# In projection of a hybrid decoder block: three passes of 256 columns become one of 512 and one of 256

## The chip, the cores and the metric

The kernel runs on one core of a Trainium2 chip. The metric is the device time of one execution in microseconds (us), as the median of several runs. All numbers are float32 at the interface.

## The reference, cut to what matters

One layer on x of 256 tokens by 2048 features:

```
proj = x @ w_in                                   # 2048 -> 4688 columns
u_ssm, q, k, v, qi, ki, wi = split(proj)          # 1024, 1024, 256, 256, 1024, 64, 16
y_ssm  = s5_mixer(u_ssm, ...)                     # diagonal state space scan, then a gated unit (GLU)
y_attn = dsa_attention(q, k, v, qi, ki, wi * c)   # indexer picks 64 keys per query, then softmax attention
h = layer_norm(alpha * x + concat(y_ssm, y_attn) @ w_out)
f = (gelu(causal_conv3(h @ w_up)) * (h @ w_gate)) @ w_down
out = layer_norm(alpha * h + f)
```

## The kernel before, in words

Every matrix product keeps nearly float32 accuracy by splitting: a float32 value is written as a high part (rounded to the engine's fp32r type) and a low part (the rest), and a product a*b is taken as high*high + high*low + low*high. Weights come from memory in halves of 128 x 1024 values (eight blocks of 128 input features for 128 output columns). `fetch` (L126) does this for one half: SyncE starts the DMA into `raw`, ScalarE writes `wh` (L133), VectorE writes `wl` (L136). Three `raw` buffers and four each of `wh` and `wl` go round, so a few halves are prepared ahead of TensorE.

x is split in the same way at the start (`load_x`, L224, with `split`, L180): its four tiles hold, for each of 16 blocks of input features, 256 columns (tokens) of the high part and right behind them 256 of the low part. The tiles arrive in this order: half of tile 0, half a weight half, the other halves of both, then tile 1, three weight halves, tile 2, tile 3.

The in projection makes 27 transposed tiles (output columns on partitions, 256 tokens along the row): eight of u for the state space part, eight of qi and one of kw for the indexer, two of k, eight of q. The v columns are done the other way round and are not touched by the change. A transposed tile takes 16 blocks, and for each block `mm3` (L184) issues three passes of 256 columns: high weights on high x (L186), low weights on high x (L187), high weights on low x (L188). All three add up in the same 256 columns of a PSUM bank. The tile is then moved to SBUF by one ScalarE copy (L303, or L315 for u, or at L626 for kw).

The first four u tiles run with all first halves before all second halves, since x's second half comes late. From the fifth on, `ws_tile` (L288) runs a tile, and after every block it calls `pump`, which issues one step of background work: first the state space job `ssm` (four blocks: matmuls `bu`, a long run of VectorE operations L561 to L575 with the results `t1a`, `t2a` or `t12b`, and matmuls L594 on those results), later the indexer (matmuls L650, ScalarE L656, VectorE L661 to L670). The names `t1a` and so on repeat every second block, so "the third block" uses `t1a` and `t2a` again.

The order on each engine is not the order of the code. A scheduler lays out all instructions engine by engine before the run; weight fetches and the moves out of PSUM are marked as of high priority. Each engine then takes its instructions strictly in that order, and waits where an operand is not there yet. Two PSUM banks named `acc` take turns over the tiles.

The up and gate products of the feed-forward part already use another scheme, `wide_half` (L195): since the high and low parts of the activations lie side by side, one pass with the high weights runs over 512 columns (high x in the first 256 columns of the bank, low x in the second 256), and one pass with the low weights runs over the 256 high columns into the first 256. The eight high passes of a half stand together, and so do the eight low ones. Its result lies in two halves of a bank, and is put together by a ScalarE copy (L1046) and a VectorE add (L1047).

Of the kernel before, what the change touches and what calls it, by code (L numbers as in the profile page):

```python
# [11 lines left out]
F32R = mybir.dt.float32r  # L12
# [70 lines left out]
def block_kernel(ctx: ExitStack, tc: tile.TileContext, x_t, x_n, prm_d, cst_d, ssm_d, w_in_d, w_kw_d, w_v_d,  # L83
# [106 lines left out]
    def act_tiles(what):  # L190
        return [(t[:, :, 0, :], t[:, :, 1, :])
                for t in (ahl.tile([P, 4, 2, S], F32R, name=f"{what}{j}", tag=f"hl{j}") for j in range(4))]

    def wide_half(out, half, tiles, kh):


        def passes(low):
            for k in range(8):
                r = tiles[(kh * 8 + k) // 4][:, k % 4]
                yield low, half[low][:, k * P:(k + 1) * P], r[:, 0] if low else r  # L200

        steps = list(passes(1)) + list(passes(0)) if kh else list(passes(0)) + list(passes(1))
        for i, (low, w, r) in enumerate(steps):
            ins = T.matmul(out[:, 0] if low else out, lhsT=w, rhs=r, start=kh == 0 and i == 0, stop=kh == 1 and i == 15)  # L204
        return ins.ins

    def kt_of(tiles, kt):
        h, l = tiles[kt // 4]
        return h[:, kt % 4, :], l[:, kt % 4, :]
# [8 lines left out]
    st = tmp.enter_context(pool("ssmt", side="right"))  # L218
    xt = act_tiles("x")
    raw_b = st.tile([P, 2, 512], F32, name="raw_b", tag="t3")  # L220
# [51 lines left out]
    def acc_tile():  # L272
        return ps.tile([P, 512], F32, name="acc", bufs=2)
# [14 lines left out]
    def ws_tile(evac, m=P):  # L288

        acc = acc_tile()  # L290
        for kt in range(16):
            if kt % 8 == 0:
                half = next_half()
            c = (kt % 8) * m
            mm3(acc[:m, :S], (half[0][:, c:c + m], half[1][:, c:c + m]), kt_of(xt, kt), kt == 0, kt == 15)
            pump()
        with tc.high_priority():
            evac(acc)

    def proj_tile(name, t=None):  # L300
        if t is None:
            t = proj.tile([P, S], F32, name=name)
        ws_tile(lambda acc: A.activation(t, acc[:, :S], AF.Copy))  # L303
        return t
# [8 lines left out]
    def u_tile(ct, acc):  # L313
        t = proj.tile([P, 2, P], F32, name=f"u{ct}")
        A.activation(t.rearrange("p two k -> p k two"), acc[:, :S].rearrange("p (k two) -> p k two", two=2), AF.Copy)  # L315
        ut.append(t)

    bu = psb.tile([P, 2, 2, 512], F32, name="bu")
    accs = [acc_tile(), acc_tile(), bu[:, 0, 0], bu[:, 0, 1]]
    for kh in range(2):  # L320
        for ct in range(4):
# [4 lines left out]
            if (kh, ct) == (1, 3):  # L326
                load_some(raw_c.rearrange("p a b -> p (a b)"), ssm_d[:, 1024:], 0, 1024)
                load_some(cst, cst_d, CST_FIRST, NCST)
            for k in range(8):
                kt = kh * 8 + k  # L330
                c = k * P
                mm3(accs[ct][:, :S], (half[0][:, c:c + P], half[1][:, c:c + P]), kt_of(xt, kt), kt == 0, kt == 15)
            if kh:
# [291 lines left out]
    kw = proj.tile([P, S], F32, name="kw")[0:80]  # L625
    ws_tile(lambda acc: A.activation(kw, acc[:80, :S], AF.Copy), m=80)  # L626
    ki2 = proj.tile([P, S], F32, name="ki2")
# [142 lines left out]

    hl_tiles = [ahl.tile([P, 4, 2, S], F32R, name=f"mix{j}", tag=f"hl{j}") for j in range(4)]
    hl = [(t[:, :, 0, :], t[:, :, 1, :]) for t in hl_tiles]
    mix = [hl[0], hl[1], mix[2], hl[3]]
# [264 lines left out]
    with pool("pd", space=PSUM) as pd:  # L1038
        for f in range(NF):
            pu = []  # L1040
            for which in range(1 if f < 4 else 2):
# [3 lines left out]
                t = ff.tile([P, S], F32, name=f"sum{which}", bufs=2)  # L1045
                A.activation(t, p[:, 1], AF.Copy)  # L1046
                V.tensor_tensor(t, t, p[:, 0], op=ALU.add)  # L1047
                pu.append(t)
# [196 lines left out]
```

## Time and profile before

| what | value |
|---|---|
| median of 3 runs | 1109.63 us (1107.95 to 1109.7) |
| the profiled execution's own time | 1110.08 us |
| its span, first to last instruction | 1108.3 us |
| TensorE (PE) busy | 1089.2 us, 98% |
| VectorE (DVE) busy | 739.4 us, 67% |
| ScalarE (ACT) busy | 578.7 us, 52% |
| DMA | 204.44 MB, mean 184 GB/s |
| mean granted TensorE clock | 0.994 of full |

PE is the engine of matmuls, PEld its weight loads, which overlap with it. Matmul rows overlap each other, because a matmul's duration reaches from its start to the end of its result: the time that a matmul takes of the engine is read from one start to the next, not from its duration. In the same way two VectorE rows that follow each other overlap a little.

### The profile page before, as it was taken

How to read it: one execution, taken by the hardware profiler on the slowest of the kernel's cores; microseconds unless marked ns; L12 is line 12 of the kernel's file. 1: busy time of each engine (PE TensorE's matmuls, PEld its weight loads, DVE VectorE, ACT ScalarE, POOL GpSimd, SP SyncE). 2: the span in 40 equal slices, each digit the busy share in tenths (PEclk: the TensorE clock that was granted, in tenths of full speed). 3: DMA queues.
4: the chain of work that ended last, by engine and by line, in shares of the span. 5: the costliest groups of instructions: out<-in, count | busy, mean ns of one | idle time of the engine just before them, and what ended most of it. 6: DMA issues, size and time to landing. Idle time of an engine off the chain costs nothing.

```text
span 1108.3 us, 16859 instructions
## 1 busy us (share of the span) xinstructions
PE 1089.2 (98%) x6576; PEld 945.8 (85%) x6576; DVE 739.4 (67%) x1044; ACT 578.7 (52%) x876; POOL 0.2 (0%) x4
## 2 busy tenths in 40 slices
PE   8999999999999999999999999999999999999995
PEld 6999998899778788888888888888888888888884
DVE  6979889687558666677666656565656556565547
ACT  5975564457544755555554545454545445454430
POOL 0000000000000000000000000000000000000000
PEclk9999999999999999999999999999999999999998
DMA  7654435346466465555755555555555566665622
GB/s 254 224 154 136 129 132 170 97 140 241 160 221 208 164 201 188 190 189 190 265 191 190 190 191 189 189 191 191 187 190 187 180 229 220 222 222 196 194 100 76
DMA packets 59311, 204.44 MB, mean 184 GB/s; under 512 B 7264, under 2 KB 10080, under 8 KB 58592
## 3 DMA queue, kind: packets, MB, share of 16 engines
q1 hardware_dynamic: 59232, 203.38, 55.2%
q8 instruction: 51, 0.84, 0.3%
q14 instruction: 28, 0.23, 0.1%
HBM read 200.20 MB, written 2.10 MB: 183 GB/s over the span
## 4 chain that ended last, share of the span: by engine, by line
PE 85%; DVE 6%; DMA 3%; ACT 2%; issue 2%; SPq 1%; DVEq 0%; ACTq 0%
PE pd L204 42%; PE e L186 7%; PE e L188 7%; PE e L187 7%; PE o L188 3%; PE o L186 3%; PE o L187 3%; PE acc L187 3%; PE acc L188 3%; PE acc L186 3%; DMA raw<-in_w_in_dram 2%; DVE wl L136 2%; PE misc L650 1%; SPq L530 1%; ACT wh L133 1%
## 5 line engine op out<-in xcount | busy, mean ns | idle before, releaser
L136 DVE TENSOR_TENSOR wl<-raw,wh 128x1024 fp32r<-128x1024 f32 x299 | 364.7, 1222 | 250.1 <-ACT wh L133 247.5
L133 ACT ACTIVATE wh<-raw 128x1024 fp32r<-128x1024 f32 x299 | 315.6, 1056 | 252.2 <-PE pd L204 138.5
L204 PE MATMUL pd<-mix,wh 128*128 128x512 f32 x1344 | 321.4, 391 | 0.7 <-ACT gate L1018 0.7
L204 PEld LDWEIGHTS pd<-mix,wh 128*128 128x128 f32 x1344 | 246.8, 188 | 48.8 <-ACT gate L1018 1.1
L204 PEld LDWEIGHTS pd<-mix,wl 128*128 128x128 f32 x1344 | 172.5, 191 | 6.6
L204 PE MATMUL pd<-mix,wl 128*128 128x256 f32 x1344 | 174.8, 283 | 0.0
L186 PE MATMUL acc<-x,wh 128*128 128x256 f32 (+1 forms) x400 | 115.2, 289 | 2.4 <-ACT x L181 1.6
L187 PE MATMUL acc<-x,wl 128*128 128x256 f32 (+1 forms) x400 | 115.9, 290 | 1.2 <-DVE wl L136 0.8
L188 PE MATMUL acc<-x,wh 128*128 128x256 f32 (+1 forms) x400 | 115.4, 289 | 0.8 <-DVE x L182 0.8
L136 DVE TENSOR_TENSOR wxl<-raw,wxh 128x1024 fp32r<-128x1024 f32 x42 | 51.4, 1225 | 44.6 <-ACT wxh L133 42.6
L186 PEld LDWEIGHTS acc<-x,wh 128*128 128x128 f32 (+1 forms) x400 | 76.8, 193 | 4.7 <-ACT x L181 1.8
L187 PEld LDWEIGHTS acc<-x,wl 128*128 128x128 f32 (+1 forms) x400 | 77.2, 193 | 4.0 <-issue 1.4
L188 PEld LDWEIGHTS acc<-x,wh 128*128 128x128 f32 (+1 forms) x400 | 77.2, 193 | 3.3 <-issue 1.6
L133 ACT ACTIVATE wxh<-raw 128x1024 fp32r<-128x1024 f32 x42 | 44.6, 1061 | 55.9 <-DMA raw<-in_w_down_dram 24.2
L187 PE MATMUL e<-wh,acthl 128*128 128x512 f32 x152 | 59.1, 389 | 0.0
L186 PE MATMUL e<-wh,acthl 128*128 128x512 f32 x152 | 59.0, 389 | 0.0
L188 PE MATMUL e<-wl,acthl 128*128 128x512 f32 x152 | 58.3, 389 | 0.0
L175 ACT ACTIVATE hc<-hc 128x256 f32<-128x256 f32 x44 | 18.4, 417 | 76.4 <-DVE hc L1060 76.4
L186 PE MATMUL e<-wxh,acthl 128*128 128x512 f32 x128 | 49.8, 389 | 0.0
L187 PE MATMUL e<-wxh,acthl 128*128 128x512 f32 x128 | 49.8, 389 | 0.0
L188 PE MATMUL e<-wxl,acthl 128*128 128x512 f32 x128 | 49.8, 389 | 0.0
L1047 DVE TENSOR_TENSOR sum<-sum,pd 128x256 f32<-128x256 f32 x84 | 34.7, 413 | 0.0
(289 smaller groups left out, 1439.4 us busy)
## 6 DMA issues: line engine op xcount, KB each, us to landing
raw<-in_w_gate_dram SPq DMA_DIRECT2D x88, 512.0 KB, 4.1
raw<-in_w_up_dram SPq DMA_DIRECT2D x88, 512.0 KB, 4.0
raw<-in_w_down_dram SPq DMA_DIRECT2D x88, 512.0 KB, 4.6
raw<-in_w_in_dram SPq DMA_DIRECT2D x51, 512.0 KB, 4.3
raw<-in_w_out_dram SPq DMA_DIRECT2D x32, 512.0 KB, 4.1
raw<-in_w_glu_dram SPq DMA_DIRECT2D x8, 512.0 KB, 3.7
raw<-in_w_v_dram SPq DMA_DIRECT2D x4, 512.0 KB, 4.2
z<-in_x_n_dram SPq DMA_DIRECT2D x1, 2048.0 KB, 8.7
```

Source lines behind the costliest of these rows:

```text
L133: A.activation(h[:, :w], raw[:, :w], AF.Copy)
L136: V.tensor_sub(l[:, :w], raw[:, :w], h[:, :w].bitcast(F32))
L175: ins = A.activation(*args, **kw)
L186: T.matmul(out, lhsT=lh[0], rhs=rh[0], start=start, stop=False)
L187: T.matmul(out, lhsT=lh[1], rhs=rh[0], start=False, stop=False)
L188: return T.matmul(out, lhsT=lh[0], rhs=rh[1], start=False, stop=stop).ins
L204: ins = T.matmul(out[:, 0] if low else out, lhsT=w, rhs=r, start=kh == 0 and i == 0, stop=kh == 1 and i == 15)
L530: nc.sync.dma_start(out=ustk[r:r + 32, c, h, :], in_=ut[2 * bi + c][32 * q:32 * q + 32, 1 - e, :])
L650: T.matmul(banks[e][:, (hp % 2) * w:(hp % 2 + 1) * w], lhsT=qit[hp][r, b * 128:(b + 1) * 128], rhs=ki2[r, 0:w], start=True, stop=True)
L1047: V.tensor_tensor(t, t, p[:, 0], op=ALU.add)
```

## The change

The transposed tiles of the in projection go over to the scheme of the up and gate products. `wide_half` gets the tile's width `m` (80 for kw) and a call `beside`, which it makes after each low pass; `ws_tile` passes `pump` there. Each tile then has 16 passes of 512 columns with the high weights and 16 of 256 with the low ones, in runs of eight: in a tile's first half the high ones first, in the second half the low ones first. The move out of PSUM becomes a ScalarE copy and a VectorE add (`add_parts`).

```diff
     def act_tiles(what):
-        return [(t[:, :, 0, :], t[:, :, 1, :])
-                for t in (ahl.tile([P, 4, 2, S], F32R, name=f"{what}{j}", tag=f"hl{j}") for j in range(4))]
-
-    def wide_half(out, half, tiles, kh):
+        return [ahl.tile([P, 4, 2, S], F32R, name=f"{what}{j}", tag=f"hl{j}") for j in range(4)]
+
+    def both_parts(tiles):
+        return [(t[:, :, 0, :], t[:, :, 1, :]) for t in tiles]
+
+    def wide_half(out, half, tiles, kh, m=P, beside=lambda: None):
 
 
         def passes(low):
             for k in range(8):
                 r = tiles[(kh * 8 + k) // 4][:, k % 4]
-                yield low, half[low][:, k * P:(k + 1) * P], r[:, 0] if low else r
+                yield low, half[low][:, k * m:(k + 1) * m], r[:, 0] if low else r
 
         steps = list(passes(1)) + list(passes(0)) if kh else list(passes(0)) + list(passes(1))
         for i, (low, w, r) in enumerate(steps):
             ins = T.matmul(out[:, 0] if low else out, lhsT=w, rhs=r, start=kh == 0 and i == 0, stop=kh == 1 and i == 15)
+            if low:
+                beside()
         return ins.ins
+
+    def two_parts(bank, m=P):
+        return bank[:m].rearrange("p (two s) -> p two s", two=2)
+
+    def add_parts(t, hi, lo):
+        A.activation(t, lo, AF.Copy)
+        V.tensor_tensor(t, t, hi, op=ALU.add)
...
     def ws_tile(evac, m=P):
 
-        acc = acc_tile()
-        for kt in range(16):
-            if kt % 8 == 0:
-                half = next_half()
-            c = (kt % 8) * m
-            mm3(acc[:m, :S], (half[0][:, c:c + m], half[1][:, c:c + m]), kt_of(xt, kt), kt == 0, kt == 15)
-            pump()
+        acc = two_parts(acc_tile(), m)
+        for kh in range(2):
+            wide_half(acc, next_half(), x_tiles, kh, m, pump)
         with tc.high_priority():
             evac(acc)
 
     def proj_tile(name, t=None):
         if t is None:
             t = proj.tile([P, S], F32, name=name)
-        ws_tile(lambda acc: A.activation(t, acc[:, :S], AF.Copy))
+        ws_tile(lambda acc: add_parts(t, acc[:, 0], acc[:, 1]))
         return t
...
     def u_tile(ct, acc):
         t = proj.tile([P, 2, P], F32, name=f"u{ct}")
-        A.activation(t.rearrange("p two k -> p k two"), acc[:, :S].rearrange("p (k two) -> p k two", two=2), AF.Copy)
+        add_parts(t, *(acc[:, i].rearrange("p (k two) -> p two k", two=2) for i in range(2)))
         ut.append(t)
 
     bu = psb.tile([P, 2, 2, 512], F32, name="bu")
-    accs = [acc_tile(), acc_tile(), bu[:, 0, 0], bu[:, 0, 1]]
+    accs = [two_parts(a) for a in (acc_tile(), acc_tile(), bu[:, 0, 0], bu[:, 0, 1])]
...
-            for k in range(8):
-                kt = kh * 8 + k
-                c = k * P
-                mm3(accs[ct][:, :S], (half[0][:, c:c + P], half[1][:, c:c + P]), kt_of(xt, kt), kt == 0, kt == 15)
+            wide_half(accs[ct], half, x_tiles, kh)
...
-    ws_tile(lambda acc: A.activation(kw, acc[:80, :S], AF.Copy), m=80)
+    ws_tile(lambda acc: add_parts(kw, acc[:, 0], acc[:, 1]), m=80)
```

The scheduler lays the program out anew. On PE, the first half of the first tile, right behind the warming matmuls, starts like this before (`x_81` is x's tile 0, `x_82` its tile 1):

```order
L186 MATMUL acc<-x_81,wh 128x256
L187 MATMUL acc<-x_81,wl 128x256
L188 MATMUL acc<-x_81,wh 128x256
L186 MATMUL acc<-x_81,wh 128x256
L187 MATMUL acc<-x_81,wl 128x256
L188 MATMUL acc<-x_81,wh 128x256
```

and like this after, where the first four rows are the whole half and the next four the half after it:

```order
L206 MATMUL acc<-x_81,wh 128x512 x4
L206 MATMUL acc<-x_82,wh 128x512 x4
L206 MATMUL acc<-x_81,wl 128x256 x4
L206 MATMUL acc<-x_82,wl 128x256 x4
L206 MATMUL acc<-x_81,wh 128x512 x4
L206 MATMUL acc<-x_82,wh 128x512 x4
```

The low passes on tile 0 of x now stand behind the high passes on tile 1, and every high pass reads both parts of x.

On VectorE, in the third block of the state space job, the order from the scan into `t2a` to the result `t1a` and a little beyond is this before (L568 is a scan, L570 to L574 the turning back, `t_1256` and `t_1257` are work tiles):

```order
L568 SCALAR_TENSOR_TENSOR t2a<-dec,t1a 128x1024
L569 SCALAR_TENSOR_TENSOR t_1257<-dec,t_1256 128x1024
L570 TENSOR_TENSOR t1a<-t2a,cs 128x1024
L136 TENSOR_TENSOR wl<-raw,wh 128x1024
L571 TENSOR_TENSOR t_1256<-t_1257,cs 128x1024
L573 TENSOR_TENSOR t2a<-t2a,cs 128x1024
L572 TENSOR_TENSOR t1a<-t1a,t_1256 128x1024
L136 TENSOR_TENSOR wl<-raw,wh 128x1024
L574 TENSOR_TENSOR t_1257<-t_1257,cs 128x1024
```

and this after (five lines further down in the code; L216 is the new add, here of the k tiles):

```order
L573 SCALAR_TENSOR_TENSOR t2a<-dec,t1a 128x1024
L216 TENSOR_TENSOR kv<-kv,acc 128x256
L574 SCALAR_TENSOR_TENSOR t_1116<-dec,t_1115 128x1024
L136 TENSOR_TENSOR wl<-raw,wh 128x1024
L575 TENSOR_TENSOR t1a<-t2a,cs 128x1024
L576 TENSOR_TENSOR t_1115<-t_1116,cs 128x1024
L578 TENSOR_TENSOR t2a<-t2a,cs 128x1024
L136 TENSOR_TENSOR wl<-raw,wh 128x1024
L577 TENSOR_TENSOR t1a<-t1a,t_1115 128x1024
```

One add and one more weight conversion stand between the scan and `t1a`, and each add waits there for the ScalarE copy of a tile that TensorE has finished.

## Rows read from the trace of the kernel before

**Rows 1.** The page: the span, busy time, and the chain that ended last.
```profile
span 1108.3 us, 16859 instructions
...
PE 1089.2 (98%) x6576; PEld 945.8 (85%) x6576; DVE 739.4 (67%) x1044; ACT 578.7 (52%) x876; POOL 0.2 (0%) x4
...
PE 85%; DVE 6%; DMA 3%; ACT 2%; issue 2%; SPq 1%; DVEq 0%; ACTq 0%
```
**Rows 2.** The three longest waits of PE from 25 to 230 us: total, times, longest.
```profile
PE acc L186 <- ACT kv L691: 0.9, 1, 0.9
PE acc L187 <- DVE wl L136: 0.8, 2, 0.5
PE bu L186 <- ACT u L315: 0.4, 1, 0.4
```
**Rows 3.** Stretches: length, busy us of PE, PEld, DVE, ACT, POOL; PE clock, DMA.
```profile
75.00:100.00 25.00, 24.49 (x306) 22.38 (x305) 25.00 (x23) 17.02 (x34) 0.00 (x0) 1.00 0.40 124
100.00:125.00 25.00, 25.00 (x281) 22.80 (x281) 23.79 (x20) 12.26 (x29) 0.00 (x0) 1.00 0.48 142
```
**Rows 4.** Groups by line and form: the L186 passes of the transposed tiles.
```profile
L186 PE MATMUL acc<-x,wh 128*128 128x256 f32 x384 | 110.7, 290 | 2.4 <-ACT x L181 1.6 <-ACT kv L691 0.9
L186 PE MATMUL bu<-x,wh 128*128 128x256 f32 x32 | 9.2, 286 | 0.4 <-ACT u L315 0.4
L186 PE MATMUL acc<-x,wh 128*80 128x256 f32 x16 | 4.5, 282 | 0.0
```
**Rows 5.** PE in order of time (start us, us), 48 passes apart.
```profile
109.35 0.28 PE L186 MATMUL acc<-x,wh 128*128 128x256 f32 x1
...
115.11 0.28 PE L186 MATMUL acc<-x,wh 128*128 128x256 f32 x1
```
**Rows 6.** PE in order of time, in the up and gate products.
```profile
504.54 3.82 PE L204 MATMUL pd<-mix,wh 128*128 128x512 f32 x16
508.19 2.08 PE L204 MATMUL pd<-mix,wl 128*128 128x256 f32 x16
510.11 3.82 PE L204 MATMUL pd<-mix,wh 128*128 128x512 f32 x16
```
**Rows 7.** Groups by line: moves out of PSUM, here and in the feed-forward part.
```profile
L1047 DVE TENSOR_TENSOR sum<-sum,pd 128x256 f32<-128x256 f32 x84 | 34.7, 413 | 0.0
L1046 ACT ACTIVATE sum<-pd 128x256 f32<-128x256 f32 x84 | 30.4, 362 | 0.0
L303 ACT ACTIVATE q<-acc 128x256 f32<-128x256 f32 x8 | 3.1, 385 | 9.8 <-PE acc L188 9.8
```
**Rows 8.** PE in order of time, at the start.
```profile
9.47 0.28 PE L188 MATMUL acc<-x,wh 128*128 128x256 f32 x1
11.31 0.38 PE L186 MATMUL acc<-x,wh 128*128 128x256 f32 x1 [1.56 <-ACT x L181]
12.57 0.38 PE L188 MATMUL acc<-x,wh 128*128 128x256 f32 x1 [0.76 <-DVE x L182]
```
**Rows 9.** VectorE at the same time: the low part of x's tile 1.
```profile
11.29 1.23 DVE L182 TENSOR_TENSOR x<-xraw,x 128x1024 fp32r<-128x1024 f32 x1
```
**Rows 10.** Stretches at the start, columns as in rows 3.
```profile
12.50:16.20 3.70, 3.63 (x18) 3.63 (x19) 3.21 (x11) 1.08 (x2) 0.00 (x0) 0.55 0.77 248
16.20:25.00 8.80, 8.80 (x75) 8.80 (x75) 7.29 (x21) 6.03 (x6) 0.00 (x0) 0.99 0.79 278
```
**Rows 11.** VectorE in order of time: start of block one, and of block three.
```profile
69.49 1.22 DVE L561 TENSOR_TENSOR t1a<-bu,cos 128x1024 f32<-128x1024 f32 x1 [2.77 <-PE bu L551]
...
128.12 0.82 DVE L136 TENSOR_TENSOR wl<-raw,wh 128x640 fp32r<-128x640 f32 x1 [3.87 <-ACT wh L133]
129.16 1.23 DVE L561 TENSOR_TENSOR t1a<-bu,cs 128x1024 f32<-128x1024 f32 x1 [0.22 <-ACT cs L175]
...
148.27 1.22 DVE L572 TENSOR_TENSOR t1a<-t1a,t 128x1024 f32<-128x1024 f32 x1
```
**Rows 12.** PE in order of time: the matmuls on the third block's `t1a`.
```profile
149.60 0.43 PE L594 MATMUL misc<-t1a,cbd 128*32 128x128 f32 x8
```

More of the change, by code (lines that the diff above doesn't have):

```diff
@@ L218, in block_kernel @@
     st = tmp.enter_context(pool("ssmt", side="right"))
-    xt = act_tiles("x")
+    x_tiles = act_tiles("x")
+    xt = both_parts(x_tiles)
     raw_b = st.tile([P, 2, 512], F32, name="raw_b", tag="t3")
@@ L768, in block_kernel @@
     drain()
-    hl_tiles = [ahl.tile([P, 4, 2, S], F32R, name=f"mix{j}", tag=f"hl{j}") for j in range(4)]
-    hl = [(t[:, :, 0, :], t[:, :, 1, :]) for t in hl_tiles]
+    hl_tiles = act_tiles("mix")
+    hl = both_parts(hl_tiles)
     mix = [hl[0], hl[1], mix[2], hl[3]]
@@ L1045, in block_kernel @@
                 t = ff.tile([P, S], F32, name=f"sum{which}", bufs=2)
-                A.activation(t, p[:, 1], AF.Copy)
-                V.tensor_tensor(t, t, p[:, 0], op=ALU.add)
+                add_parts(t, p[:, 0], p[:, 1])
                 pu.append(t)
```

## The prediction

> **What bounds the kernel now.** I read the page first, then the waits of PE over the in projection, then the stretches, then rows in order of time. The page shows PE busy 98% of the span and PE with 85% of the chain that ended last [rows 1]. That alone doesn't make PE the limit, since a matmul's row can cover a stall, so I looked at what PE waits for: from 25 to 230 us, where nearly all of the in projection lies, the three longest entries come to 2.1 us, with 0.8 us of it for low weights and 0.4 us for a move out of PSUM [rows 2]. So PE's own passes set the pace of this stage, and time taken from them is time taken from the end, as long as nobody else becomes late. The one who might is VectorE: it is busy 25.00 us of 25 from 75 to 100 us and 23.79 us from 100 to 125 us [rows 3], because there it runs the state space scans beside the weight conversions. The change takes work from PE and gives work to VectorE, in the one stage in which VectorE is full. The prediction is the balance of the two.
>
> **Passes.** The transposed tiles have 384 + 32 + 16 = 432 blocks [rows 4], that is 27 tiles of 16. A block has three passes, a tile 48. Forty-eight passes without a gap take 115.11 - 109.35 = 5.76 us [rows 5], 0.120 us each. The new form is seen in the up and gate products: 16 wide passes take 508.19 - 504.54 = 3.65 us (0.228 us each) and 16 narrow ones 510.11 - 508.19 = 1.92 us, a tile 5.57 us [rows 6]. The product has as many columns as before; what goes is one start of a pass per block, 2 x 0.120 - 0.228 = 0.012 us. A tile gains 5.76 - 5.57 = 0.19 us, 27 of them 5.1 us. Nearest rows for what the wide form costs in other hands: none is closer than these, with the same tile layout and the same scheme, so I take 5.1 us, and as bounds 4.5 and 5.3 us, by the rounding of the starts.
>
> The Trainium skill, page "TensorE: Matmul & The Clock Gate", section "Back-to-back issue gap", speaks against this term: it gives a matmul of N columns N / 2.4 + 2.5 ns, so that merging two passes would save 2.5 ns, an estimate of 27 x 16 x 2.5 ns = 1.1 us for the whole change. The trace doesn't agree: a pass of 256 columns takes 120 ns from start to start, and not the 109 ns of the formula, and one of 512 takes 228 ns, not 216 [rows 5, 6].
>
> **The start.** The first half of the first tile now has its four high passes on x's tile 1 ahead of all low passes, and each of these reads tile 1's low part, which VectorE ends at 11.29 + 1.23 = 12.52 us [rows 9]. Before, PE had issued 12 passes by 9.47 us and two more from 11.31 us, and went on at 12.57 us with the fifteenth [rows 8], so 10 of 24 were left. After, only four wide passes can be done by 12.52 us, and four wide and eight narrow are left, 16 narrow ones' worth. Six more are due: at 0.120 us that is 0.7 us; but from 12.5 to 16.2 us the granted clock was 0.55 of full, nearly the lower of the two levels (1.2 of 2.4 GHz), with 18 passes in 3.70 us, 0.21 us each [rows 10], and at that rate it is 1.3 us. The low clock follows a PE that was mostly idle, and it will be idle longer now. The bounds are 0.7 us and 1.3 us and another 1.7 us if the low clock lasts for 18 passes more (18 x 0.09). I take 0.9 us, since at least part of these passes will run slowly.
>
> **Moves out of PSUM.** Each of the 27 tiles had one ScalarE copy of 0.385 us and now has a copy of 0.362 us and an add on VectorE of 0.413 us, by the same pair in the feed-forward part [rows 7]; the adds come to 27 x 0.41 = 11 us, or 27 x 0.33 = 9 us from start to start. On PE's path they cost nothing where two `acc` banks take turns: a bank has a tile's 5.57 us to be emptied, and copy and add need 0.8 us. That cover is gone where VectorE's queue is further behind than 4.8 us, and it cannot jump its queue. What stands behind an add on VectorE are weight conversions and the state space run; who waits for them is PE, in its own strict order.
>
> **VectorE in the state space part.** Here is the place where the added work can come out. From the start of the first block (69.49 us) to the third block's `t1a` (148.27 + 1.22 = 149.49 us) VectorE had 80.0 us, with idle time in it, and PE took up `t1a` at 149.60 us, 0.1 us after it was ready [rows 11, 12]. By the new order nine adds lie in that stretch: 9 x 0.33 to 9 x 0.41, 3.0 to 3.7 us. Counted in the order, PE has 10.4 tiles between the two points before and as much after, which now take 10.4 x 0.19 = 2.0 us less. So PE would come 2.0 us sooner for something that is 3.3 us later, 5.2 us of wait with the slack of 0.1 us taken off. Against that stands idle time of VectorE before the third block, 3.87 us for high weights of kw and 0.22 us for a table [rows 11]; in the new order both kw conversions stand among operations of the second block, so that VectorE has something else to do. If all of it is used, 5.2 - 4.1 = 1.1 us of wait is left, if none, 5.2 us; below nothing it can't be, except that the wait is spared. I take 1.2 us, since the 3.87 us row is the one that the new order visibly fills.
>
> **Low weights.** The 0.8 us of waits for low weights [rows 2] stood where PE wanted them in a block's second pass. In a first half they are now wanted 8 x 0.228 = 1.8 us after the first pass, in a second half at once. One of the two waits was in a first half; I take 0.6 us off for it, with the restart of the pipeline, bounds 0 and 1.2 us.
>
> **Sum.** -5.1 + 0.9 + 1.2 - 0.6 = -3.6 us. From the profiled execution's 1110.08 us (1.8 us more than its span, lying outside it, and left as it is) that makes 1106.5 us. The runs' median is 0.45 us below that execution, so for a median I predict 1106.0 us. All later stages hang on PE's end of this one, so the gain moves through them undiminished: in the glu products and behind them, VectorE has the rest of its added work to do, but with the chain on PE [rows 1].
>
> **Rivals.** (a) The gain is swallowed: VectorE's lag costs all it can, 5.2 us in place of 1.2 us, at the third block's `t1a`. For it: VectorE full in rows 3, PE only 0.1 us behind it in rows 12. Against: idle time to be filled. Time: 1106.0 + 4.0 = 1110.0 us. The skill's formula ends nearly there for another reason (no gain per pass), and the rows just given are against it; I count it in here with little weight.
> (b) VectorE sets the pace of the whole stretch, slower than before. Each new add makes VectorE wait for the ScalarE copy of a tile that PE has only just ended; if VectorE reaches each of the nine adds a microsecond early, it idles 9 us in all, its run to `t1a` gets 9 + 3.3 us longer, and with the 2.0 us and 4.1 us as above PE waits 10.3 us there: 1106.0 - 1.2 + 10.3 = 1115.1 us. It decides from 0.6 us of idle time per add on, where the result is a loss of over 2 us. For it: the queue is strict. Against: VectorE is full, so it rather comes late to an add than early.
> (c) The full gain: no wait at `t1a`, the start costs 0.7 us, both waits for low weights go: -5.1 + 0.7 - 1.2 = -5.6 us, 1104.0 us. For it: the scheduler has placed `t1a` anew. Against: the slack of 0.1 us.
>
> **How the numbers follow.** A change below 0.2%, 2.2 us, can't be told from none here. My forecast (1104.8 to 1107.6 us) has a chance of 0.45, (c) and what lies below 0.17, (a) with all small gains and losses 0.27, (b) 0.11. Of the forecast's own share nearly nine tenths lie under 1107.4 us. So faster 0.59, the same 0.30, slower 0.11. The range of 8 in 10 leaves out (b) and the best part of (c): 1103.4 to 1111.0 us.
>
> **What would show it.** Right: the transposed tiles as 432 wide and 432 narrow passes with starts 0.228 and 0.120 us apart; the start's first wide pass on x's tile 1 behind 12.5 us; a wait of PE of about a microsecond for `t1a` of the third block, or a row that covers it; 27 adds of 0.41 us on VectorE; the end of the last in projection tile 3 to 4 us earlier. Wrong: PE idle before `acc` matmuls for an add (an `acc` bank freed late), rows of VectorE adds with idle time for ScalarE ahead of them, or wide passes further apart than 0.228 us.

## The result, and the profile after

The changed kernel takes 1117.32 us (median of 6 runs, 1113.55 to 1119.16), the kernel before 1108.85 us beside it (6 runs). The ratio is 1.0075, with an interval of [1.0061, 1.0089]: 8.5 us slower. Predicted were 1106.0 us and a range up to 1111.0 us. The profiled execution took 1118.05 us, 7.97 us more than the one of before.

The page of the changed kernel: span, busy time, and shares of the chain that ended last, which answer to [rows 1].

```profile
span 1116.2 us, 16022 instructions
...
PE 1089.2 (98%) x6144; PEld 923.9 (83%) x6144; DVE 748.4 (67%) x1071; ACT 577.6 (52%) x876; POOL 0.2 (0%) x4
...
PE 85%; DVE 6%; DMA 4%; ACT 2%; issue 2%; SPq 1%; DVEq 0%; ACTq 0%
```

PE has 432 matmuls fewer and the same busy time, 1089.2 us. The span has grown by 7.9 us, so PE's idle time has: 19.1 us before, 27.0 us after. That the busy time didn't fall by the gain of the passes is put down to the clock further below, in an estimate. PE's passes themselves, in order of time (start us, us), are what the prediction took from the up and gate products [rows 6]:

```profile
114.92 3.79 PE L206 MATMUL acc<-x,wh 128*128 128x512 f32 x16
118.55 0.64 PE L206 MATMUL acc<-x,wl 128*128 128x256 f32 x4
...
190.67 2.08 PE L206 MATMUL acc<-x,wl 128*128 128x256 f32 x16
192.59 0.39 PE L206 MATMUL acc<-x,wh 128*128 128x512 f32 x1
```

Sixteen wide ones take 3.63 us from start to start (3.65 predicted), sixteen narrow ones 1.92 us (1.92). Now the waits of PE from 25 to 230 us (total, times, longest), which answer to [rows 2]:

```profile
PE acc L188 <- DVE wl L136: 2.5, 1, 2.5
PE acc L206 <- ACT kv L696: 2.2, 1, 2.2
PE acc L206 <- DVE wl L136: 1.3, 2, 0.8
PE bu L556 <- DMA ustk<-u: 0.9, 1, 0.9
```

They come to 6.9 us, where the three longest of before came to 2.1 us and all five of before to 2.7 us. Stretches of the changed kernel (length, busy us of PE, PEld, DVE, ACT, POOL with counts, then the granted clock, DMA share, GB/s):

```profile
80.00:85.60 5.60, 4.64 (x156) 3.96 (x155) 5.60 (x5) 3.35 (x10) 0.00 (x0) 1.00 0.46 127
85.60:92.40 6.80, 6.80 (x22) 5.68 (x23) 6.80 (x8) 4.05 (x12) 0.00 (x0) 0.50 0.25 78
157.30:160.70 3.40, 3.40 (x22) 2.79 (x22) 3.40 (x5) 1.56 (x6) 0.00 (x0) 0.50 0.52 151
174.30:177.70 3.40, 3.40 (x9) 2.63 (x10) 3.40 (x4) 1.25 (x3) 0.00 (x0) 0.50 0.00 0
```

And of the kernel before:

```profile
85.60:92.40 6.80, 6.80 (x58) 6.80 (x58) 6.80 (x7) 5.37 (x7) 0.00 (x0) 1.00 0.32 98
157.30:160.70 3.40, 3.40 (x62) 2.57 (x50) 0.74 (x1) 2.56 (x5) 0.00 (x0) 1.00 0.56 188
169.90:173.30 3.40, 3.40 (x17) 3.18 (x16) 3.40 (x4) 1.14 (x2) 0.00 (x0) 0.50 0.72 247
```

The clock fell to its lower level (1.2 of 2.4 GHz) for 3.4 us near 170 us before, and does so near 174 us after; new are 85.6 to 92.4 us and 157.3 to 160.7 us. With the one at the start and without the end of the run these stretches are 6.8 us long before and 17.0 us after. If PE works at half rate in them, an estimate, they cost 3.4 and 8.5 us; the narrow passes below, 0.21 us apart in place of 0.12 us, make it 44% of the length rather than half, and the difference 4.5 us rather than 5.1 us. With that the account of the two profiled executions closes within 0.6 us: -5.1 us of passes, +4.5 to +5.1 us of low clock, +7.9 us of idle PE, against the +7.9 us of the span. It is an estimate for this pair and not a rule: it misses e16, below, by 4.7 us. The 0.989 of mean clock is no accident of one execution: the share of full clock that is missing, times the span, was 12.1 us in the mean over six runs of the changed kernel, and 5.9 us over the 25 runs of the kernel before that stand beside e1.

PE ahead of two of the low stretches and in the first of them (start us, us; idle time and its releaser in brackets; the passes at 157.42 and 159.13 us are eight starts apart), and VectorE with the low weight that PE waits for:

```profile
156.90 0.39 PE L188 MATMUL acc<-wl,x 128*128 128x256 f32 x1 [2.45 <-DVE wl L136]
...
157.42 0.41 PE L188 MATMUL acc<-wl,x 128*128 128x256 f32 x1
...
159.13 0.41 PE L187 MATMUL acc<-wh,x 128*128 128x256 f32 x1
...
174.12 1.49 PE L206 MATMUL acc<-x,wh 128*128 128x512 f32 x3 [2.23 <-ACT kv L696]
```

```profile
154.49 1.22 DVE L578 TENSOR_TENSOR t2a<-t2a,cs 128x1024 f32<-128x1024 f32 x1
155.62 1.22 DVE L136 TENSOR_TENSOR wl<-raw,wh 128x1024 fp32r<-128x1024 f32 x1
156.76 1.22 DVE L577 TENSOR_TENSOR t1a<-t1a,t 128x1024 f32<-128x1024 f32 x1
```

The weight of a v half stands in VectorE's queue between products of the third block, and that block is late. How late, and since when, shows further up in VectorE's order of time after, beside [rows 11]:

```profile
58.25 0.69 DVE L472 TENSOR_TENSOR raw_b<-uvB 128x512 f32<-128x512 f32 x1
...
73.04 1.23 DVE L566 TENSOR_TENSOR t1a<-bu,cos 128x1024 f32<-128x1024 f32 x1 [2.91 <-PE bu L556]
...
130.31 0.70 DVE L363 TENSOR_SCALAR cs<-cs 128x1024 f32<-128x1024 f32 x1 [1.11 <-ACT cs L358]
136.99 1.23 DVE L566 TENSOR_TENSOR t1a<-bu,cs 128x1024 f32<-128x1024 f32 x1 [2.15 <-ACT cs L175]
```

Before, the row for `raw_b` was this one, on the same engine:

```profile
54.47 0.69 DVE L467 TENSOR_TENSOR raw_b<-uvB 128x512 f32<-128x512 f32 x1
```

`raw_b` is what the first block's weights are made from; in VectorE's queue it is 3.8 us late, behind six adds of u tiles. The first block starts 3.5 us late (69.49, now 73.04), the third 7.8 us (129.16, now 136.99), and its `t1a` is ready at 157.98 us, 8.5 us late. That the first delay hands on the second is not shown. PE transposes what is made of `raw_b` (L500, now L505) and multiplies by it (`bu`); here is PE from the first of these transposes to the first `bu`, before and after:

```profile
57.41 0.38 PE L500 MATMUL misc<-cst,bbd 128*128 128x128 f32 x2
...
64.81 0.49 PE L551 MATMUL bu<-ustk,bt 64*128 64x128 f32 x2
```

```profile
57.99 0.38 PE L505 MATMUL misc<-cst,bbd 128*128 128x128 f32 x2
...
69.50 1.82 PE L556 MATMUL bu<-ustk,bt 64*128 64x128 f32 x26
```

PE comes to the transposes only 0.6 us later and waits for nothing in between. It comes to `bu` 4.7 us later mainly because the new order has more of the in projection ahead of it: 50 narrow passes before, 6.0 us at 0.12 us each, and 32 wide and 20 narrow ones after, 9.7 us. So the first block's start was moved by the order on PE; whether the scheduler chose this order because of the adds is open. Where the lag comes out behind the in projection: PE after, in the o products, and the indexer's second mask `nm` on VectorE, after and before.

```profile
276.74 0.66 PE L744 MATMUL misc<-cst,e 128*128 128x128 f32 x4 [0.92 <-DVE e L723]
...
347.01 0.47 PE L186 MATMUL o<-wqh,mix 128*128 128x512 f32 x1 [1.00 <-DVE z L854]
```

```profile
273.25 0.29 DVE L674 TENSOR_SCALAR nm<-score 128x256 f32<-128x256 f32 x1
```

```profile
242.95 0.29 DVE L669 TENSOR_SCALAR nm<-score 128x256 f32<-128x256 f32 x1
```

The mask is ready 30 us later, behind the start of the o products (265.7 us), and the `e` that PE waits for at 276.74 us is made from it. Up to the last GLU matmul the changed kernel has lost 4.0 us, from there to the first matmul of the up products 3.8 us more, 2.4 us of it idle PE, and nothing behind.

### The profile page after: what moved, and what is told of

It is laid out like the page before. It is cut to its first block, busy times and chain, and to the rows that moved or that the text cites. A ratio compares the mean times of both kernels' runs of the same rounds, so it can differ in the third digit from the quotient of the medians.

```text
span 1116.2 us, 16022 instructions
## 1 busy us (share of the span) xinstructions
PE 1089.2 (98%) x6144; PEld 923.9 (83%) x6144; DVE 748.4 (67%) x1071; ACT 577.6 (52%) x876; POOL 0.2 (0%) x4
## 4 chain that ended last, share of the span: by engine, by line
PE 85%; DVE 6%; DMA 4%; ACT 2%; issue 2%; SPq 1%; DVEq 0%; ACTq 0%
PE pd L206 42%; PE acc L206 8%; PE e L186 7%; PE e L187 7%; PE e L188 7%; PE o L186 2%; PE o L187 2%; PE o L188 2%; DVE wl L136 1%; DMA raw<-in_w_out_dram 1%; PE misc L655 1%; DMA xraw<-in_x_t_dram 1%; PE acc L186 1%; PE acc L188 1%; PE acc L187 1%
## 5 line engine op out<-in xcount | busy, mean ns | idle before, releaser
L206 PE MATMUL acc<-x,wh 128*128 128x512 f32 (+1 forms) x400 | 105.0, 408 | 6.1 <-DVE x L182 3.9
L206 PEld LDWEIGHTS acc<-x,wh 128*128 128x128 f32 (+1 forms) x400 | 74.6, 194 | 24.6 <-DVE x L182 4.7
L206 PE MATMUL acc<-x,wl 128*128 128x256 f32 (+1 forms) x400 | 58.5, 293 | 1.3 <-DVE wl L136 1.3
L206 PEld LDWEIGHTS acc<-x,wl 128*128 128x128 f32 (+1 forms) x400 | 54.0, 195 | 6.4 <-DVE wl L136 1.7
L186 PE MATMUL e<-wh,acthl 128*128 128x512 f32 x152 | 59.0, 389 | 0.0
L186 PE MATMUL e<-wxh,acthl 128*128 128x512 f32 x128 | 49.8, 389 | 0.0
L216 DVE TENSOR_TENSOR sum<-sum,pd 128x256 f32<-128x256 f32 x84 | 34.8, 414 | 0.0
L188 PEld LDWEIGHTS e<-wl,acthl 128*128 128x128 f32 x152 | 28.5, 188 | 6.0
L186 PEld LDWEIGHTS e<-wh,acthl 128*128 128x128 f32 x152 | 28.5, 188 | 6.0
```

The lines of the kernel that those rows point to most:

```text
L186: T.matmul(out, lhsT=lh[0], rhs=rh[0], start=start, stop=False)
L188: return T.matmul(out, lhsT=lh[0], rhs=rh[1], start=False, stop=stop).ins
L216: V.tensor_tensor(t, t, hi, op=ALU.add)
```

## The experiments

Theory V, at first: the adds make VectorE late, and PE waits behind it. Rival O: the passes in runs of eight, with all background steps behind low passes, leave stretches in which PE has only thin work. The table has all runs; "ratio" is to the kernel before on the same chip; "clock" is the missing share of full clock times the span, in us, as mean over the runs. The last three columns are from the profiled execution: start of the first block on VectorE, and the delay against the profile of before at the last GLU matmul and at the first up matmul. They hold for that execution alone: the profiled one was the shortest of e1 (1110.45 us) and of e9 (1108.56 us), and the longest of e2, e12 and e14.

| run | median us | ratio | clock | first block | GLU end | up start |
|---|---|---|---|---|---|---|
| before | 1109.3 | | 5.9 | 69.5 | 0 | 0 |
| changed | 1117.3 | 1.0075 [1.0061, 1.0089] | 12.1 | 73.0 | +4.0 | +7.8 |
| e1_adds_alone | 1112.25 | 1.0026 [1.0016, 1.0036] | 6.7 | 70.0 | +0.2 | +0.4 |
| e2_passes_alone | 1109.09 | 1.0002 [0.9990, 1.0014] | 7.9 | 70.7 | -0.3 | +2.6 |
| e3_by_blocks | 1108.19 | 0.9996 [0.9987, 1.0004] | 7.5 | 72.5 | -3.7 | -2.1 |
| e4_gpsimd_adds | 1112.75 | 1.0037 [1.0023, 1.0051] | 9.8 | 71.5 | +1.6 | +3.3 |
| e5_spread | 1114.84 | 1.0054 [1.0041, 1.0068] | 9.7 | 72.7 | +3.0 | +5.4 |
| e6_eights_alone | 1107.36 | 0.9990 [0.9980, 1.0001] | 6.7 | 68.3 | -4.2 | -3.4 |
| e7_blocks_sbuf | 1111.63 | 1.0028 [1.0017, 1.0038] | 9.7 | 72.5 | -0.3 | +2.4 |
| e8_blocks_gpsimd | 1109.33 | 1.0000 [0.9988, 1.0013] | 9.8 | 71.4 | -0.8 | +0.7 |
| e9_spare_adds | 1113.63 | 1.0038 [1.0021, 1.0055] | 14.8 | 86.6 | -4.9 | -1.7 |
| e10_wl_gpsimd | 1112.93 | 1.0032 [1.0021, 1.0044] | 10.0 | 72.8 | +0.7 | +2.7 |
| e11_blocks_wl_gpsimd | 1117.05 | 1.0069 [1.0056, 1.0082] | 10.0 | 71.8 | +5.6 | +5.6 |
| e12_before_wl_gpsimd | 1122.38 | 1.0117 [1.0102, 1.0133] | 8.4 | 69.5 | +13.2 | +14.4 |
| e13_u_old | 1113.31 | 1.0036 [1.0023, 1.0050] | 8.7 | 68.3 | -1.0 | +3.4 |
| e14_u_new | 1110.61 | 1.0005 [0.9992, 1.0018] | 6.9 | 70.3 | +0.1 | +2.8 |
| e15_blocks_u_old | 1110.90 | 1.0019 [1.0006, 1.0031] | 10.2 | 70.8 | +0.4 | +2.5 |
| e16_u_copy | 1108.83 | 0.9999 [0.9989, 1.0008] | 9.0 | 70.3 | -4.0 | -0.6 |
| e17_u_gpsimd | 1115.68 | 1.0064 [1.0042, 1.0085] | 10.4 | 72.2 | +0.5 | +6.0 |
| e18_blocks_u_gpsimd | 1113.32 | 1.0039 [1.0025, 1.0053] | 10.0 | 72.6 | +3.0 | +4.1 |

**The change taken apart (e1 to e4).** e1, the kernel before with the third pass in the bank's second half, and copy and add:

```diff
+    def mm3_apart(out, lh, rh, start, stop):
...
+        return T.matmul(out[:, 1], lhsT=lh[0], rhs=rh[1], start=False, stop=stop).ins
...
-        ws_tile(lambda acc: A.activation(t, acc[:, :S], AF.Copy))
+        ws_tile(lambda acc: add_parts(t, acc[:, 0], acc[:, 1]))
...
```

> The three narrow passes per block of before, in before's order, with the high-weights-on-low-x pass summed in the second half of the bank, so that only the move out of PSUM is the new one (ScalarE copy and VectorE add). Theory V (VectorE's added work makes it late, and PE waits behind it): of the 13 us between the 5.1 us saved on passes and the 7.9 us lost in the profiled spans, 1.0 us is the start and 3.4 us the low clock from 85.6 to 92.4 us; the other 8.6 us belong to the adds, so about 1109 + 8.6 = 1117 to 1118 us. Theory O (the runs of eight and the background steps bunched between low passes cost the time): no longer than before by more than 1 us, 1108 to 1110 us.

e2, the changed kernel without adds:

```diff
-        ws_tile(lambda acc: add_parts(t, acc[:, 0], acc[:, 1]))
+        ws_tile(lambda acc: A.activation(t, acc[:, 0], AF.Copy))
...
```

> The changed kernel with its new passes, but the move out of PSUM is one ScalarE copy of the first half of the bank: the second half, the product of high weights and low x, is left out of the in projection's transposed tiles. Theory V: the 8.6 us go, 1108 to 1109 us, and if the low clock from 85.6 to 92.4 us goes with them 1105 us. Theory O: 1116 to 1117.5 us, nothing gained but the adds' own short waits.

e3, the changed kernel with both passes of a block side by side and a background step behind each block:

```diff
+    def wide_blocks(out, half, tiles, kh, m=P, beside=lambda: None):
+        for k in range(8):
+            r = tiles[(kh * 8 + k) // 4][:, k % 4]
+            for low in range(2):
+                T.matmul(out[:, 0] if low else out, lhsT=half[low][:, k * m:(k + 1) * m], rhs=r[:, 0] if low else r,
+                         start=kh == 0 and k == 0 and not low, stop=kh == 1 and k == 7 and bool(low))
+            beside()
...
```

> The changed kernel with wide and narrow pass of one block side by side and a background step after each block, as mm3 had it, also in the first four tiles; the adds stay. Theory V: the start gets 0.5 us better and nothing else, 1116 to 1117 us. Theory O: the start and the low clock at 85.6 us are won back, 4 us or more, 1112 to 1113 us.

e4, the changed kernel with two ScalarE copies (the lower part's goes into `part`) and the add on GpSimd:

```diff
+    def add_beside(t, hi, lo):
...
+        A.activation(t, hi, AF.Copy)
+        G.tensor_tensor(whole, whole, part, op=ALU.add)
...
-        ws_tile(lambda acc: add_parts(t, acc[:, 0], acc[:, 1]))
+        ws_tile(lambda acc: add_beside(t, acc[:, 0], acc[:, 1]))
...
```

> The changed kernel with the add on GpSimd: ScalarE copies both halves of the bank out (0.36 us more of it per tile, 27 x 0.36 = 10 us on an engine that is 52% busy), GpSimd, which is idle, adds them. Theory V: VectorE is as free as before, so 1107 to 1110 us, less what a slow GpSimd add delays. Theory O: as the changed kernel, 1116 to 1118 us.

The adds alone cost 3.0 us, not the whole loss; the passes without adds gain nothing; both together cost 8.5 us in the changed kernel, and nothing in e3. In e1 the waits of PE from 25 to 230 us begin with an add that a bank waits for:

```profile
PE acc L186 <- DVE kv L201: 1.7, 1, 1.7
PE acc L192 <- ACT kv L704: 1.4, 1, 1.4
```

They are of an execution that was only 0.4 us longer than the profiled one of before, so no profile shows where e1's 3.0 us lie.

e2 has what the changed kernel has, without an add, and its profiled execution (its longest, 1112.8 us) shows where the passes' gain goes:

```profile
PE acc L206 <- ACT u L323: 1.5, 1, 1.5
PE bu L556 <- DMA ustk<-u: 1.4, 1, 1.4
PE bu L206 <- ACT u L323: 1.1, 1, 1.1
PE acc L206 <- ACT kv L696: 0.9, 1, 0.9
```

```profile
84.30:94.50 10.20, 10.20 (x35) 8.32 (x34) 9.89 (x10) 5.35 (x14) 0.00 (x0) 0.50 0.17 58
```

PE is quicker through its passes and waits for others, 24.3 us of idle time in place of 19.1 us, and 10.2 us of low clock follow. Its twelve runs range with the clock: four with 0.990 or 0.991 took 1110.8 to 1112.8 us, the eight with 0.993 to 0.997 took 1105.1 to 1109.8 us.

**The order of the passes and the background (e5, e6).** e3 is 9 us faster than the changed kernel with the same passes and adds, so the order was suspected. In the mean over the runs, 4.6 of the 9 us are the clock's (12.1 and 7.5 us).

```diff
-            if low:
+            if i % 2:
                 beside()
```

> The changed kernel with one edit: the background step follows every second pass of the sixteen of a half, the high ones too, instead of every one of the eight low passes; passes, their order and the adds stay. Measured so far: before 1109.3, changed 1117.3, adds alone 1112.3, passes without adds 1109.1, wide and narrow of one block side by side 1108.2. Theory B (bunched background): with a step behind each low pass only, TensorE does a stretch of background steps and thin passes and then a stretch of dense ones; the granted clock falls behind the thin stretches (in the changed kernel it is 0.5 from 85.6 to 92.4 us and from 157.3 to 160.7 us, in the kernel before at neither place). Then spreading the same steps over all passes brings back most of it: 1108 to 1111 us, and a granted clock of 0.992 or more. Theory L (the order of the passes itself: eight high ones and then eight low ones, and so the times at which weights and adds are wanted): the time stays at 1115 to 1118 us.

e6, the kernel before with its three narrow passes in runs of eight:

```diff
-            mm3(acc[:m, :S], (half[0][:, c:c + m], half[1][:, c:c + m]), kt_of(xt, kt), kt == 0, kt == 15)
-            pump()
+        for kh in range(2):
+            by_eights(acc[:m, :S], next_half(), kh, m, pump)
...
```

> The kernel before with one edit: its three passes of 256 columns and its single copy out of PSUM stay, but a half's blocks go eight of a kind (high weights with both parts of x for eight blocks, then the low weights for eight, the other way round in the second half), with the background step behind each low pass, as in the changed kernel. No wide pass, no add. Theory B (bunched background): slower than the kernel before by 3 to 7 us, 1112 to 1116 us, with more low granted clock before 200 us. Rival A (the order costs only where VectorE's adds stand on it, since passes without adds took the time of the kernel before): no change, 1108 to 1111 us.

Spreading the steps brings back 2.5 us of 8.5, and the low stretches and the waits of e5 are those of the changed kernel, within 0.5 us. Runs of eight cost nothing with narrow passes and one copy. So the order is no cause by itself, and theory B falls. But it matters together with the adds: e3 has the changed kernel's passes and adds and none of its loss.

**The bank or VectorE's queue (e7 to e9).** In e3 the waits are for adds:

```profile
PE acc L215 <- DVE qi L224: 2.6, 2, 2.2
PE acc L186 <- DVE kv L224: 1.9, 1, 1.9
```

e7 and e8 are e3 with the edit of e4, the add of e7 on VectorE (`V` for `G`).

> Wide and narrow pass of one block side by side (1108.2 us measured), and the tile leaves its bank by two ScalarE copies, the high part's into a spare tile; VectorE adds the two in the scratchpad, in place of adding from the bank. VectorE's count of instructions is unchanged; only the release of the bank no longer stands behind VectorE's queue. In the side by side kernel TensorE waits 2.6 us on qi and 1.9 us on kv moves of VectorE. Theory P (the bank is held until VectorE gets to the add): those waits go, 1103 to 1106 us. Rival Q (VectorE's queue has 27 more instructions and all that is behind them is late, whatever the bank does): 1107 to 1109 us.

> As the one with two ScalarE copies, but the add in the scratchpad is on GpSimd: VectorE has none of the 27 adds. Theory P (the bank is held until VectorE gets to the add): the same as with the add on VectorE, within 1 us, 1103 to 1106 us. Rival Q (VectorE's queue is what is late): 1102 to 1105 us, and 3 us or more below the one with the add on VectorE. A third possibility is that the GpSimd add, 2 to 3 us each in the run of the changed kernel with such adds, brings u or kv late to its reader: 1107 to 1110 us.

The expectations of e9 to e12 call "third" the block that starts at 162.1 us before and at 170.0 us after; in the count used elsewhere here it is the fourth. e9 is e2 with an add on a spare tile behind each copy:

```diff
+    def spare_add():
+        V.tensor_tensor(spare[:, 0], spare[:, 0], spare[:, 1], op=ALU.add)
...
```

> The kernel with the new passes and one copy (1109.1 us; high weights with the low part of x left out of the result), and behind each tile's copy one VectorE add of 128x256 on a spare tile that nothing reads: VectorE's queue is as long as in the changed kernel, but no bank and no reader stands behind an add. Theory V (VectorE's queue is what comes late: its third state-space block starts at 162.1 us in the kernel before, 164.7 with the new passes and one copy, 170.0 in the changed kernel): 1114 to 1117 us, the third block's start at 168 us or later. Rival P (what costs is the bank, or the tile, that waits for its add): 1108 to 1111 us.

Neither e7 nor e8 gained: with banks freed by ScalarE the time is 3.4 us above e3, and with no adds on VectorE either it is 1.1 us above, within the intervals of both. e9 is between its theories and tells little: its first block started at 86.6 us, so the scheduler had moved far more than the adds, and its loss to the clock was the largest of all.

**VectorE relieved elsewhere (e10 to e12).** `BESIDE` is every third of the weight halves 18 to 39.

```diff
-                V.tensor_sub(l[:, :w], raw[:, :w], h[:, :w].bitcast(F32))
+                (G if n in BESIDE else V).tensor_sub(l[:, :w], raw[:, :w], h[:, :w].bitcast(F32))
```

> The changed kernel with eight of the subtractions that make low weights (every third of the halves 18 to 39; 1.22 us each on VectorE, 9.8 us in all) on GpSimd, which is idle there; the 27 adds stay on VectorE. VectorE's load is then about that of the kernel before. Theory V (VectorE's queue): most of what the change lost comes back, 1105 to 1110 us, the third block's start at 164 us or earlier. Rival P (the bank or the tile waits for its add): 1114 to 1118 us. A low weight that GpSimd makes too slowly would show as a wait of TensorE for wl on GpSimd.

> Wide and narrow pass of one block side by side (1108.2 us) with the same eight subtractions on GpSimd. Theory V: the third block's start comes from 165.4 to 160 us or earlier, 1102 to 1105 us, a version below the kernel before. Rival P: 1107 to 1109 us.

> The kernel before with the same eight subtractions on GpSimd, as the control: what a shorter VectorE queue is worth without the change. Theory V, if VectorE's blocks already set the pace there: the third block's start from 162.1 to 155 us or so, 1104 to 1107 us. If TensorE's passes set the pace in the kernel before (as the prediction had it): 1107 to 1110 us, no change, while the changed kernel gains by the same edit.

With this edit the changed kernel gains 4.4 us, about half its loss; the other two lose 9 and 13 us. In e12 PE stands for the conversion itself, and for a copy:

```profile
PE acc L188 <- POOL wl L137: 4.1, 1, 4.1
PE misc L589 <- ACT dd L586: 3.0, 1, 3.0
```

So the relief is mixed with a new wait in the controls, and only e10, where PE doesn't wait for GpSimd, speaks for theory V. VectorE's blocks are still late there; the longest wait of PE from 25 to 230 us in e10 is for one:

```profile
PE misc L600 <- DVE t1a L578: 2.9, 1, 2.9
```

**Which tiles (e13 to e18).** Theory U read the rows of `raw_b` so that the u tiles' adds stand at the head of the lag. e13 and e15 give the eight u tiles to the old form (`mm3` with `pump` behind each block, one copy), e14 the other 19:

```diff
-        ws_tile(lambda acc: u_tile(ct, acc))
+        old_tile(lambda acc: u_tile(ct, acc))
...
```

> The changed kernel with the eight u tiles in the old way (three passes of 256 columns, one copy), and the other 19 tiles as changed. Theory U (the u tiles' adds delay what the first state-space block is made from): the first block starts on VectorE at 70 us or before (73.0 in the changed kernel), the third at 131 to 134 us (137.0), and the time is 1108 to 1112 us, though 8 x 0.19 = 1.5 us of the passes' gain is given up. Theory R (the adds inside the blocks): 1114 to 1118 us.

> The kernel before with only the eight u tiles in the new way, and the other 19 as before. Theory U: the first block starts on VectorE at 72 us or later, and the time is 1111 to 1115 us, most of the loss with 8 of 27 adds. Theory R: 1107 to 1110 us.

> The u tiles in the old way, the other 19 with wide and narrow pass of one block side by side (that order in all 27 tiles: 1108.2 us). Theory U: the first block back at 70 us or before, and 1103 to 1107 us, below the kernel before (1109.0). Theory R: 1107 to 1110 us.

e16, one copy for the u tiles, all else as changed:

```diff
-        add_parts(t, *(acc[:, i].rearrange("p (k two) -> p two k", two=2) for i in range(2)))
+        A.activation(t, acc[:, 0].rearrange("p (k two) -> p two k", two=2), AF.Copy)
```

> The changed kernel without the eight adds of the u tiles (one copy of the bank's first half; the product of high weights with the low part of x is left out of u), with all passes and the other 19 adds. Theory U: 1109 to 1112 us, 5 us or more below the changed kernel, the first block's start at 71 us or before. Theory R: 1115 to 1118 us.

e17 and e18 have the edit of e4 for u tiles alone, on the changed kernel and on e3.

> The changed kernel with the eight u adds on GpSimd (two ScalarE copies, the add in the scratchpad, about 2 us each in the run with all adds there); the other 19 adds stay on VectorE. If the u adds cost by their place in VectorE's queue: 1108 to 1111 us, the first block's start at 71 us or before. If a u tile that is late by an add is what costs: 1114 to 1118 us.

> Wide and narrow pass of one block side by side (1108.2 us with all adds on VectorE) with the eight u adds on GpSimd. If the u adds cost by their place in VectorE's queue: 1104 to 1108 us, a version below the kernel before (1109.1). If not, or if this order of passes has no loss left for them to cause: 1108 to 1111 us.

Taking eight of 27 adds out of the changed kernel takes out all of the loss (e16, -8.5 us). It doesn't take out PE's waits. From the page of e16:

```profile
span 1107.9 us, 16012 instructions
...
PE 1079.4 (97%) x6144; PEld 916.9 (83%) x6144; DVE 743.7 (67%) x1063; ACT 576.1 (52%) x876; POOL 0.2 (0%) x4
```

PE is idle for 28.5 us there, against 27.0 us in the changed kernel. The low stretches, without the end of the run, are 6.8 us long again, 10.2 us less than in the changed kernel, which by the estimate above is worth 4.5 to 5.1 us; the rest lies in PE's busy time and isn't explained, so some of what a row counts as busy may be waiting too.

The other runs don't bear theory U out either: the u tiles alone in the new form cost 1.3 us, which is not told from none (e14), the other 19 alone 4.0 us (e13), and the same adds on GpSimd, with VectorE's queue relieved as in e16, leave 6.6 us (e17). On the order of e3, the old form (e15) and GpSimd (e18) for the u tiles take 2.7 and 5.1 us longer than e3 itself. In e13 the first block is back at 68.3 us and the third at 129.5 us, as in the kernel before, and the time is lost behind them: PE waits 2.7 us for the gate of the GLU ahead of the o products, and the clock is low from 263.6 to 267.1 us.

```profile
PE o L186 <- ACT sgm L175: 2.7, 1, 2.7
```

In e17 the waits from 25 to 230 us begin with the second of the two copies that free a bank (L222), and an add of k:

```profile
PE bu L206 <- ACT u L222: 2.5, 1, 2.5
PE acc L186 <- DVE kv L216: 1.7, 1, 1.7
```

Nor does the first block's start order the times: it is 1.9 to 3.2 us late in e4, e7, e8, e17 and e18, where `raw_b` starts by 54.9 us, and 0.5 us late in e1, where `raw_b` starts at 58.4 us as in the changed kernel; e3, with the block 3.0 us late, has no loss, and e13, with it early, 4.0 us. No version beat the kernel before: the best, e6, has an interval that reaches to 1.0001.

## Why the prediction was wrong, step by step

**"PE's own passes set the pace of this stage, and time taken from them is time taken from the end".** This is the step that failed. It was read from 2.1 us of waits in 205 us, and e2 is its test: the same 5.1 us off PE's passes, no add on anything, and a ratio of 1.0002 [0.9990, 1.0014]. The small waits said that nobody was late for PE, not that anybody could be quicker: with quicker passes, PE in e2 waits for copies of u, for transfers and for kv, and is idle for 5.2 us more than before.

**Passes, -5.1 us.** Right as PE's work: 3.63 and 1.92 us for 3.65 and 1.92. Wrong as time at the end.

**The start, +0.9 us.** Right. PE waited 2.87 us at its first pass on x's tile 1, in this order of time (answers to [rows 8]), and the half after the first one began at 15.65 us in place of 14.62, 1.0 us later:

```profile
9.29 0.73 PE L206 MATMUL acc<-x,wh 128*128 128x512 f32 x2 [1.00 <-DVE x L182]
12.90 1.25 PE L206 MATMUL acc<-x,wh 128*128 128x512 f32 x4 [2.87 <-DVE x L182]
```

**Moves out of PSUM, nothing on PE's path.** Wrong: adds with everything else as before cost 3.0 us (e1), and PE stood 1.7 us for one of them in the execution profiled.

**VectorE in the state space part, +1.2 us (1.1 to 5.2).** The mechanism was seen, in another place than forecast, and the term was too small. It began to count at the first block's start and took that as fixed; in the new order the block starts 3.5 us late. It counted nine adds, 3.0 to 3.7 us, and left out a low weight: the stretch between the two points of [rows 11] has 19 of them after and 18 before, and VectorE's busy time in it grew by 4.6 us. It took VectorE's idle time as a reserve that would be used: VectorE was idle there for 4.55 of 80.0 us before, and after for 4.92 of 84.94 us, so none was used, and the stretch grew by 4.9 us. And it looked for the wait at `t1a`: that has none, since the late low weight ahead of it had PE waiting for 2.45 us.

**Low weights, -0.6 us.** Wrong in sign: 0.8 us of waits became 3.8 us, 2.45 us of it in a v tile, which the change doesn't touch.

**"The gain moves through them undiminished".** Wrong: 3.8 of the 8 us are lost between the GLU and the up products. e16 and e2 show the same: they have 4.0 and 0.3 us in hand at the last GLU matmul, and 0.6 us and -2.6 us at the first up matmul. From there to the end every kernel keeps its place within 0.2 us, so there the sentence holds.

**The clock, not in the sum.** The prediction priced the low clock at the start alone. In the account above some 13 us stand against the passes' 5.1 us, and 4.5 to 5.1 us of them are the clock's; in the mean over runs the clock took 6.2 us more than before.

**The rivals.** The time came out near (b), 1115.1 us, but not by its mechanism: ahead of the nine adds of that stretch VectorE was idle for 0.1 us in all, where (b) wanted a microsecond each. (a) had the place right and left out the first block and the clock. (b)'s own terms add up to 10.1 us of wait, not 10.3 us, and the chance of 0.59 for faster takes more than the nine tenths that it names; neither slip changes the outcome.

What is shown: the passes' gain doesn't reach the end, even without adds; adds and passes together cost more than the sum of each alone in the changed kernel (8.5 us against 3.0 and 0), and nothing with the passes in another order (e3); without the u adds the changed kernel has no loss, though PE is idle as long. By the estimate, what was lost in its profile, some 13 us, is 4.5 to 5.1 us of low clock and 7.9 us of idle PE. Open is what makes the two parts add up to more than their sum. Each variant is laid out anew by the scheduler, and moves waits of 1 to 4 us to other places; which of these moves is due to an edit's work and which to the new order was not separated by 18 runs. An edit that keeps the order of every queue was not tried.

## What to carry to other kernels

An engine that waits little in a full stage need not be the one that sets its pace: before a gain on it is counted, ask which of the other queues could come earlier, and if none could, count the gain at nothing. When work is added to a strict queue, don't take the start of the chain that it delays as fixed, since a new order can move it, and don't take the queue's idle time as a reserve. A change that leaves TensorE less to do in such a stage can pay again by the clock, so the granted clock belongs into the sum.

## What was not expected of the hardware

Most of PE's waits of 2 us and more come with a low clock: 2.45 us before 157.3 us and 2.23 us before 174.3 us in the changed kernel, 2.7 us before 263.6 us in e13. In the twenty profiles there are 21 such waits between 16 and 390 us; in 16 of them the clock fell within the wait or at most 1.5 us behind it. In five it didn't, and these aren't only the short ones; behind this one of e9 the granted clock stayed at 1.00:

```profile
160.70 1.66 PE L206 MATMUL acc<-x,wh 128*128 128x512 f32 x6 [2.96 <-ACT kv L702]
```

Ahead of 85.6 us there was no such wait, but 156 matmuls in 5.6 us, nearly all small ones, with PE busy for 4.64 us. The kernels with narrow passes in all tiles lost 5.9 to 6.8 us to the clock in the mean (before, e1, e6), and 8.4 us with low weights made on GpSimd (e12); the thirteen with wide passes in all 27 tiles lost 7.5 to 14.8 us.

Seven of the eight subtractions on GpSimd are of whole halves. They took 3.04 us each in the mean in e10, 4.08 us in e11 and 4.96 us in e12, where VectorE takes 1.22 us; spans on GpSimd are rough in this profile.

```profile
L137 POOL TENSOR_TENSOR wl<-raw,wh 128x1024 fp32r<-128x1024 f32 x7 | 21.3, 3040 | 121.8 <-ACT wh L134 97.4 <-PE acc L207 15.1 <-DMA ustk<-u 9.4
```

```profile
L137 POOL TENSOR_TENSOR wl<-raw,wh 128x1024 fp32r<-128x1024 f32 x7 | 34.7, 4958 | 128.0 <-ACT wh L134 113.9 <-DMA raw<-in_w_in_dram 14.1
```

The first row is of e10, the second of e12 (group, busy us, mean ns, idle before). The Trainium skill, page "Trainium Architecture — The Big Picture", section "The five engines, in one table", puts streaming elementwise work on GpSimd at twice VectorE's time; here it is 2.5 to 4.1 times, and differs between kernels for the same operation.
